# Eight output tiles instead of four in the first group of each MLP's up projection

## The chip, the cores and the metric

The kernel runs on one core of a Trainium2 chip. The metric is the device time of one execution in microseconds; smaller is better. Three executions of the kernel before took 2712.76 us (median), 2692.44 us (lowest) and 2718.33 us (highest).

## The reference

One inference step of a small diffusion backbone with two trunk layers, on 128 context tokens and 128 latent tokens, all in float32 with a model width of 2048. Layer 0 mixes with differential attention and an RWKV-7 scan, layer 1 with a Conformer convolution; each is followed by a gated MLP with a depthwise convolution of width 3. Before each of the four blocks stands an RMSNorm with a shift and a scale, behind each a gate, and these come from the conditioning vectors (adaLN). Cut to what the change touches:

```python
def adaln(cvec, w, b):
    return (jax.nn.silu(cvec) @ w + b)[:, None, :]

def conv_ffn(h, w_up, w_dw, w_down):
    u = dwconv(h @ w_up, w_dw)
    gate, val = jnp.split(u, 2, axis=-1)
    return (jax.nn.silu(gate) * val) @ w_down

# per layer l
sh1, sc1, g1, sh2, sc2, g2 = jnp.split(adaln(c, w_ada[l], b_ada[l]), 6, axis=-1)
...
h = rmsnorm(x, norm_g[l, 1]) * (1.0 + sc2) + sh2
x = x + g2 * conv_ffn(h, w_up[l], w_ffn_dw[l], w_down[l])
```

w_up is 2048 x 11008 (5504 gate columns and 5504 value columns), w_down 5504 x 2048, w_ada 2048 x 12288 for each layer. The conditioning vector is a vector, so adaLN is two matrix-vector products per layer (one for the context, one for the latent tokens), and their cost is the reading of w_ada.

## The kernel before

Activations lie transposed: 128 features on the partitions, 256 columns (128 context and 128 latent tokens). A float32 operand is split into a rounded part and a remainder, so each product of a 128 x 128 weight tile with the input of one k-tile takes three matmuls of 256 columns: weight times input, weight times the input's remainder, and the weight's remainder times input (lines 252, 254, 255).

**The weight stream.** All big weights go through one stream (`emit_load`, lines 175 to 198). SyncE issues the DMAs into a ring of seven raw buffers of 1024 columns (line 188), ScalarE copies one into the weight buffer (line 192), VectorE, or GpSimd in the convolution layer, makes the remainder (line 194). There are four weight buffers of 1024 columns each. A load holds as many k-tiles as fit: two for a group of four tiles (512 columns), one for a group of eight (1024).

**A matrix product** (`gemm`, line 235) runs over its plan's groups of output tiles. For each group it takes PSUM banks (two tiles to a bank, seven banks in all), runs over the k-tiles, and for each k-tile does all tiles of the group. After each k-tile it lets waiting evacuations advance by two steps (`pump`) and calls `fill`, a hook for other work. When the group is done, its evacuation is put on the list of pending work, to be stepped during the next group.

**The MLP** (`ffn`, line 1519) is four products: up for the first 22 of 43 feature tiles (gate and value tiles of a group together), down over these 22 k-tiles, up for the other 21, and down over them. A group of an up projection has two gate and two value tiles. Its evacuation (`up_evac`, line 1523) copies each tile from PSUM with the middle tap (line 1530), adds the two other taps on VectorE (line 1535), and then makes SiLU, the product (line 1543) and the two parts of the result (lines 1545 and 1550). The buffers of line 1529 hold eight tiles.

**The input of the up projection** (`modulated`, line 558) is made one k-tile at a time while the first group runs, at most two k-tiles ahead of it: two instructions on VectorE at line 572, two on ScalarE at line 575, two on VectorE at line 577.

**The adaLN vectors** are made in small steps by one generator, `ada_gen` (line 463), in a fixed order: for layer 0 shift and scale of the mixer, gate g1, sc2, sh2, gate g2, then for layer 1 sc1, sh1, g1, sc2, sh2, g2, each but the first two in two halves of 1024 columns with 16 loads of 512 KB of w_ada. There are two ways. `ada_vec` (line 426) multiplies on VectorE, two products of 128 x 1024 per load (lines 444 and 446), one product to a call; a half takes 38 calls: one for the first load, 32 with a product, three empty, one for 16 small matmuls (line 454) and one for the transpose and the end. It is used for layer 0's g2, layer 1's sc1, sh1, g2 and the first half of layer 1's g1. `ada_pe` (line 392) uses TensorE (line 421); in layer 1 a call takes two loads, and a half takes ten calls: one that only loads, eight with matmuls, of which seven load as well, and one for the end. Both take raw buffers from the same ring and DMAs from the same SyncE queue as the weight stream.

Calls are handed out by counting k-tiles in `fill`. In the output projection of layer 0 every fourth k-tile of 28 makes a call (line 1511). In layer 0's MLP it is every second one after the sixteenth, through all four products, until the first half of layer 1's g1 is done (line 1572; k-tiles before the last four of a product with `tail=4` count). In the convolution layer's first projection (144 k-tiles) it is every fourth after the sixteenth (line 1671), and while its last evacuations drain one call a round (line 1683). Its second projection (line 1734) has no fill. In layer 1's MLP it is every second one after the sixteenth (line 1741). Where a vector is needed, `ada_until` (line 491) hands out all calls that are missing, in one block: for layer 1's sc2 and sh2 that is line 1736, between the second projection and the MLP's input.

The order that the code gives is a priority. A planner with a cost model sorts the instructions of all engines at build time and may draw work ahead when it is ready, but a raw buffer goes to the next load in order.

Of the kernel before, what the change touches and what calls it, by code (L numbers as in the profile page):

```python
# [82 lines left out]
def tile_step(ctx: ExitStack, tc: tile.TileContext, A):  # L83
# [499 lines left out]
    def view_for(wap):  # L583
        def load(eng, dst, g, kt, na):
            pieces, w = g["pieces"], g["w"]
            n = len(pieces)
            step = pieces[1] - pieces[0] if n > 1 else wap.shape[1]
            src = wap[:, 0:n * step].rearrange("(k p) (m y) -> p k m y", p=P, m=n)
            src = src[:, kt:kt + na, :, pieces[0]:pieces[0] + w]
            dst = dst.rearrange("p (a m x) -> p a m x", a=na, m=n)  # L590
            if n < na:
                for m in range(n):
                    eng.dma_start(out=dst[:, :, m], in_=src[:, :, m])
            else:
                for a in range(na):
                    eng.dma_start(out=dst[:, a], in_=src[:, a])
        return load

    def grp(pieces, w, tiles, **kw):
        return dict(pieces=pieces, w=w, n=len(pieces) * w, tiles=tiles, **kw)  # L600
# [23 lines left out]
    def ffn_plans(l):  # L624
        def ups(a, b):
            gs = []
            i = a
            while i < b:
                n = min(2, b - i)
                gs.append(grp([i * P, DFF + i * P], n * P, [P * j for j in range(2 * n)], i=i, n_=n))  # L630
                i += n
            return Plan(view_for(A["w_up"][l]), gs, list(range(KT)))

        def downs(a, b):
            return Plan(view_for(A["w_down"][l]), full, list(range(a, b)))
        return [ups(0, HALF), downs(0, HALF), ups(HALF, FT), downs(HALF, FT)]
# [1169 lines left out]
```

## Time and profile before

| | |
|---|---|
| median of three executions | 2712.76 us |
| the profiled execution, its own time | 2696.26 us |
| span of its instructions | 2694.4 us |
| mean granted clock of TensorE | 0.978 |
| TensorE busy (matmul) | 96% of the span |
| VectorE busy | 75% |
| ScalarE busy | 47% |
| GpSimd busy | 11% |
| DMA | 616.58 MB, 229 GB/s over the span |

In the profile PE is TensorE's matmuls and PEld its weight loads, DVE VectorE, ACT ScalarE, POOL GpSimd, SP SyncE with its DMA queue. A row of an engine's instructions in order of time has the start, the length, engine and line, the operation, the tile written and the tiles read, the shape, how many instructions are merged, and in brackets how long the engine sat idle before it and what ended that. Tiles go by their names in the code: `raw` is a raw buffer, `wbt` the weight buffers, `hbt` the modulated input of a product, `mm` a PSUM bank, `u` the MLP's inner activation, `av` the sums of an adaLN half on VectorE, `cu` the convolution's sums. A table of stretches gives, for each, its length, the busy time of the engines with the number of instructions that started, the granted clock, the DMA share and the rate in GB/s. Layer 0's MLP runs from 819.65 us to about 1575, the convolution layer from there to 1931.5, layer 1's MLP from about 1970 to 2674.

### The profile page before, as it was taken

How to read it: one execution, taken by the hardware profiler on the slowest of the kernel's cores; microseconds unless marked ns; L12 is line 12 of the kernel's file. 1: busy time of each engine (PE TensorE's matmuls, PEld its weight loads, DVE VectorE, ACT ScalarE, POOL GpSimd, SP SyncE). 2: the span in 40 equal slices, each digit the busy share in tenths (PEclk: the TensorE clock that was granted, in tenths of full speed). 3: DMA queues.
4: the chain of work that ended last, by engine and by line, in shares of the span. 5: the costliest groups of instructions: out<-in, count | busy, mean ns of one | idle time of the engine just before them, and what ended most of it. 6: DMA issues, size and time to landing. Idle time of an engine off the chain costs nothing.

```text
span 2694.4 us, 60352 instructions
## 1 busy us (share of the span) xinstructions
PE 2599.1 (96%) x24347; PEld 2436.0 (90%) x24347; DVE 2031.0 (75%) x3460; ACT 1258.8 (47%) x2063; POOL 300.5 (11%) x313
## 2 busy tenths in 40 slices
PE   6999998999998999999999989999999999999998
PEld 5898996667898999999999989978889999999998
DVE  3667755676579898888999989995579985566655
ACT  4335544545345444434444453355444443355544
POOL 2000112011100000000000057753200000000000
PEclk9999999999799999999999999999999999999999
DMA  9996666656366887877878857875798876666663
GB/s 299 340 290 189 190 182 233 215 197 219 109 192 195 250 269 246 275 250 248 278 248 264 273 173 245 293 233 163 245 309 267 259 234 194 193 194 196 193 190 118
DMA packets 421368, 616.58 MB, mean 229 GB/s; under 512 B 32437, under 2 KB 291864, under 8 KB 420448
## 3 DMA queue, kind: packets, MB, share of 16 engines
q1 hardware_dynamic: 416688, 600.83, 70.1%
q0 software_dynamic: 3040, 6.57, 0.7%
q10 hardware_dynamic: 1360, 5.33, 0.5%
q8 instruction: 191, 3.13, 0.5%
q14 instruction: 89, 0.73, 0.1%
HBM read 604.75 MB, written 7.86 MB: 227 GB/s over the span
## 4 chain that ended last, share of the span: by engine, by line
PE 80%; DVE 5%; DMA 3%; ACT 1%; issue 1%; POOL 1%; SPq 1%; DVEq 0%; ACTq 0%; POOLq 0%
PE mm L252 22%; PE mm L255 22%; PE mm L254 22%; PE ada L421 3%; DMA raw<-in_w_ada 2%; PE mm L1078 1%; DMA raw<-in_w_up 1%; DVE cu L1646 1%; DVE wbt L194 1%; PE mm L1639 1%; PE mm L1111 1%; DVE av L446 1%; PE mm L1115 0%; PE ada L454 0%; PE mm L1273 0%
## 5 line engine op out<-in xcount | busy, mean ns | idle before, releaser
L192 ACT ACTIVATE wbt<-raw 128x1024 fp32r<-128x1024 f32 (+3 forms) x768 | 795.2, 1037 | 1032.0 <-PE mm L254 714.6
L252 PE MATMUL mm<-hbt,wbt 128*128 128x256 f32 x3888 | 1087.5, 282 | 6.0 <-ACT hbt L575 2.3
L254 PE MATMUL mm<-hbt,wbt 128*128 128x256 f32 x3888 | 1082.3, 280 | 3.2 <-DVE hbt L577 3.2
L194 DVE TENSOR_TENSOR wbt<-raw,wbt 128x1024 fp32r<-128x1024 f32 (+1 forms) x688 | 814.0, 1189 | 351.8 <-ACT wbt L192 343.1
L255 PE MATMUL mm<-hbt,wbt 128*128 128x256 f32 x3888 | 1065.1, 281 | 5.5 <-DVE wbt L194 5.3
L252 PEld LDWEIGHTS mm<-hbt,wbt 128*128 128x128 f32 x3888 | 734.3, 189 | 20.6 <-issue 9.2
L254 PEld LDWEIGHTS mm<-hbt,wbt 128*128 128x128 f32 x3888 | 734.6, 189 | 7.3 <-DVE hbt L577 5.2
L255 PEld LDWEIGHTS mm<-hbt,wbt 128*128 128x128 f32 x3888 | 723.5, 189 | 11.2 <-DVE wbt L194 6.6
L254 PE MATMUL mm<-u,wbt 128*128 128x256 f32 x1344 | 371.3, 278 | 0.0
L252 PE MATMUL mm<-u,wbt 128*128 128x256 f32 x1344 | 371.1, 278 | 0.0
L255 PE MATMUL mm<-u,wbt 128*128 128x256 f32 x1344 | 366.0, 278 | 0.0
L446 DVE SCALAR_TENSOR_TENSOR av<-raw,silu_c,av 128x1024 f32<-128x1024 f32 x270 | 337.4, 1280 | 32.6 <-DMA raw<-in_w_ada 32.4
L194 POOL TENSOR_TENSOR wbt<-raw,wbt 128x1024 fp32r<-128x1024 f32 x80 | 193.8, 2431 | 908.5 <-ACT wbt L192 905.7
L252 PEld LDWEIGHTS mm<-u,wbt 128*128 128x128 f32 x1344 | 252.2, 188 | 0.4 <-issue 0.4
L254 PEld LDWEIGHTS mm<-u,wbt 128*128 128x128 f32 x1344 | 252.1, 188 | 0.4 <-issue 0.4
L255 PEld LDWEIGHTS mm<-u,wbt 128*128 128x128 f32 x1344 | 249.2, 188 | 0.4 <-issue 0.4
L421 PE MATMUL ada<-raw,silu_c 128*32 128x256 f32 (+2 forms) x2688 | 157.3, 338 | 31.6 <-DMA raw<-in_w_ada 25.2
L1646 DVE SCALAR_TENSOR_TENSOR cu<-mm,vec,cu 128x256 f32<-128x256 f32 x428 | 174.9, 474 | 2.3 <-ACT cu L1630 1.0
L1535 DVE SCALAR_TENSOR_TENSOR cv<-mm,vec,cv 128x254 f32<-128x254 f32 x344 | 147.5, 475 | 12.6 <-ACT cv L1530 12.6
L421 PEld LDWEIGHTS ada<-raw,silu_c 128*32 128x32 f32 x2688 | 68.0, 114 | 87.8 <-issue 28.1
L286 PE MATMUL mm<-hbt,wbt 128*128 128x256 f32 x448 | 131.6, 298 | 0.4 <-ACT hbt L575 0.4
L288 PE MATMUL mm<-hbt,wbt 128*128 128x256 f32 x448 | 127.1, 285 | 0.3 <-DVE hbt L577 0.3
(442 smaller groups left out, 2800.0 us busy)
## 6 DMA issues: line engine op xcount, KB each, us to landing
raw<-in_w_ada SPq DMA_DIRECT2D x384, 512.0 KB, 5.4
raw<-in_w_up SPq DMA_DIRECT2D x688, 256.0 KB, 4.2
raw<-in_w_down SPq DMA_DIRECT2D x168, 512.0 KB, 5.0
raw<-in_w_pw SPq DMA_DIRECT2D x128, 256.0 KB, 4.3
raw<-in_w_in SPq DMA_DIRECT2D x64, 384.0 KB, 5.7
raw<-in_w_in SPq DMA_DIRECT2D x48, 512.0 KB, 3.8
raw<-in_w_out SPq DMA_DIRECT2D x32, 512.0 KB, 4.0
raw<-in_w_pw SPq DMA_DIRECT2D x32, 512.0 KB, 4.7
```

The lines of the kernel that those rows point to most:

```text
L192: act.activation(w[:, 0, 0:na * n], v, AF.Copy)
L194: pl.lo(pl.count).tensor_tensor(out=w[:, 1, 0:na * n], in0=v, in1=w[:, 0, 0:na * n].bitcast(F32), op=ALU.subtract)
L252: pe.matmul(ps, lhsT=hi, rhs=r[:, 0:TT], start=(ki == 0 and (nl > 0 or j % 2 == 0)), stop=False, skip_group_check=True)
L254: pe.matmul(ps, lhsT=hi, rhs=r[:, TT:2 * TT], start=False, stop=False, skip_group_check=True)
L255: pe.matmul(ps, lhsT=lo, rhs=r[:, 0:TT], start=False, stop=(ki == nk - 1), skip_group_check=True)
L286: pe.matmul(ps, lhsT=hi, rhs=r[:, 0:TT], start=(ki == 0 and j % 2 == 0), stop=False, skip_group_check=True)
L288: pe.matmul(ps, lhsT=hi, rhs=r[:, TT:2 * TT], start=False, stop=False, skip_group_check=True)
L421: pe.matmul(ps[32 * j:32 * j + 32, 0:nb * 32], lhsT=silu_c[:, kt, :], rhs=rv[:, j], start=(kt == 0), stop=(kt == KT - 1))
L446: dve.scalar_tensor_tensor(out=av[:, s], in0=raw, scalar=sc, in1=av[:, s], op0=ALU.mult, op1=ALU.add)
L1078: pe.matmul(dst_[h][:, s * TT:(s + 1) * TT], lhsT=src[pr, s], rhs=kr[pr, s].rearrange("p a t -> p (a t)"), start=True, stop=True)
L1535: dve.scalar_tensor_tensor(out=o[:, :, a_], in0=v2(ps)[:, :, b_], scalar=w(k, ct), in1=o[:, :, a_], op0=ALU.mult, op1=ALU.add)
L1646: dve.scalar_tensor_tensor(out=o, in0=pads[a](k), scalar=V("w_dw", k * KT + ct), in1=o, op0=ALU.mult, op1=ALU.add)
```

## The change

The first group of the first up projection of each layer's MLP (feature tile 0) takes four gate and four value tiles. The nine groups behind it keep two and two, so the plan has ten groups for its 22 feature tiles where it had eleven. A load of the first group holds one k-tile of 1024 columns, one DMA of 512 KB with pieces of 512 columns, where it held two k-tiles of 512 columns in two DMAs of 256 KB with pieces of 256.

```diff
             while i < b:
-                n = min(2, b - i)
+                n = 4 if i == 0 else min(2, b - i)
                 gs.append(grp([i * P, DFF + i * P], n * P, [P * j for j in range(2 * n)], i=i, n_=n))
                 i += n
```

## The prediction

> **What bounds the kernel now.** I read the page's totals first, then engine busy time by stretch, then TensorE's instructions in order of time for idle before them, last SyncE's queue and VectorE in the same stretches.
>
> ```profile
> span 2694.4 us, 60352 instructions
> PE 2599.1 (96%) x24347; PEld 2436.0 (90%) x24347; DVE 2031.0 (75%) x3460; ACT 1258.8 (47%) x2063; POOL 300.5 (11%) x313
> ...
> L194 DVE TENSOR_TENSOR wbt<-raw,wbt 128x1024 fp32r<-128x1024 f32 (+1 forms) x688 | 814.0, 1189 | 351.8 <-ACT wbt L192 343.1
> ...
> L446 DVE SCALAR_TENSOR_TENSOR av<-raw,silu_c,av 128x1024 f32<-128x1024 f32 x270 | 337.4, 1280 | 32.6 <-DMA raw<-in_w_ada 32.4
> ```
> ```profile
> 815.00:1076.00 261.00, 255.10 (x2130) 251.28 (x2131) 241.61 (x344) 130.12 (x201) 0.00 (x0) 0.98 0.77 240
> ...
> 1838.00:1931.50 93.50, 93.32 (x772) 93.18 (x774) 54.89 (x95) 51.16 (x78) 41.05 (x22) 0.97 0.55 169
> 1931.50:1970.00 38.50, 28.28 (x300) 14.07 (x299) 13.03 (x48) 7.56 (x21) 0.00 (x0) 0.87 0.96 358
> 1970.00:2192.00 222.00, 221.96 (x1876) 220.78 (x1880) 213.98 (x278) 113.48 (x167) 0.00 (x0) 0.99 0.85 271
> ...
> 1860.00:1900.00 40.00, 40.00 (x342) 40.00 (x341) 20.81 (x31) 17.35 (x23) 18.96 (x9) 1.00 0.62 190
> ```
> Columns of the second fence: stretch and length, busy PE, PEld, DVE, ACT, POOL with counts, granted clock, DMA share, GB/s. TensorE is the bound nearly everywhere: 342 matmuls in 40 us are 0.117 us each, so a k-step of four tiles (12 matmuls) takes 1.40 us, of eight (24) 2.81 us, a group of four tiles 22.5 us. VectorE is close behind in the up projections (242 of 261 us and 214 of 222). One stretch is different: 1931.5 to 1970, where TensorE issues only 300 matmuls while DMA is at 0.96.
>
> ```profile
> 1931.50:1967.70 36.20, 18.69 (x240) 5.93 (x240) 0.89 0.95 359
> ```
> This is the same table for line 421 alone: the block between the convolution layer's second projection and layer 1's MLP is filled by 240 small adaLN matmuls.
>
> What can the first group of an up projection lose today? In layer 0 it starts at 819.65, in layer 1 in earnest at 1969.87:
>
> ```profile
> 819.65 0.79 PE L252 MATMUL mm<-hbt,wbt 128*128 128x256 f32 x2 [1.17 <-ACT hbt L575]
> 820.74 0.58 PE L254 MATMUL mm<-hbt,wbt 128*128 128x256 f32 x1 [0.30 <-DVE hbt L577]
> 840.18 0.39 PE L254 MATMUL mm<-hbt,wbt 128*128 128x256 f32 x1 [0.54 <-DVE hbt L577]
> 857.00 0.39 PE L255 MATMUL mm<-hbt,wbt 128*128 128x256 f32 x1 [2.65 <-DVE wbt L194]
> 1969.87 0.58 PE L252 MATMUL mm<-hbt,wbt 128*128 128x256 f32 x1 [1.58 <-ACT wbt L192]
> ```
> The waits after the start are 0.30 + 0.54 us for the modulated input and 2.65 us for a weight split: 3.5 us in layer 0. In layer 1 TensorE is busy 221.96 of 222.00 us after 1970. So there is little to win here.
>
> **The change part by part.** *Matmuls.* Their number and shapes stay; 16 steps of 24 replace 32 of 12: 0.
>
> *Start of the group.* The input of k-step kt is made while the group runs:
>
> ```profile
> 831.47 0.60 DVE L572 SCALAR_TENSOR_TENSOR ht<-x,Acoef,mm 128x128 f32<-128x128 f32 x2
> 831.99 0.87 DVE L577 SCALAR_TENSOR_TENSOR hbt<-ht,adaT,hbt 128x128 fp32r<-128x128 f32 x3
> ...
> 851.41 2.48 DVE L446 SCALAR_TENSOR_TENSOR av<-raw,silu_c,av 128x1024 f32<-128x1024 f32 x2 [1.96 <-DMA raw<-in_w_ada]
> ...
> 856.86 1.65 DVE L1535 SCALAR_TENSOR_TENSOR cv<-mm,vec,cv 128x254 f32<-128x254 f32 x4
> ...
> 863.86 0.76 DVE L1543 TENSOR_TENSOR cv<-cv 128x256 f32<-128x256 f32 x2
> ```
> Two instructions of 0.30 and two of 0.29 us a step are 1.18 us; half a weight split (1.19) makes 1.78 us against TensorE's 1.40, so VectorE falls behind by 6 us over the group, most of which the prefetched weights cover. With eight tiles it is 1.18 + 1.19 = 2.37 against 2.81: the waits for the input go. The 2.65 us stand behind an adaLN product (L446) that waited 1.96 us for its weights and kept the split at L194 waiting; the fill begins only after 16 k-steps, which are now 45 us long, so it moves away from the crowded start. I take -3.0 (bounds 0 and -3.5); in layer 1 nothing.
>
> *Loads.* Sixteen w_up DMAs of 512 KB replace 32 of 256 KB, with the same bytes per matmul; both forms fill the same four weight buffers, and before the group both stop at two loads ahead (48 matmuls): 0.
>
> *Evacuation.* All eight tiles come due in the second group: 16 of L1535 at 0.41, eight of L1543/L1550's size at 0.38, eight splits at 1.19 and 6.7 adaLN products at 1.28 make 27.7 us of VectorE in 22.5 us of TensorE (22.9 before). The cover is the lead that VectorE wins in the first group, 16 x 0.44 = 7 us: 0, and 5.2 us per layer if the lead is gone. Four banks of seven are held then, and the second group needs two: 0.
>
> *Fewer k-steps.* The up projection's first plan has 160 k-steps instead of 176, and adaLN work is handed out by counting k-steps. Layer 0's MLP has 520 now and 504 then; every second one after the sixteenth makes a step: 252 and 244. With 7 from the output projection that is 259 and 251 calls. A VectorE part takes 38 calls, so layer 0's g2 and layer 1's sc1 and sh1 (228) still fit, but layer 1's g1 first half (to 266) now lacks 15 calls instead of 7. The convolution's first projection offers (144 - 16) / 4 = 32 calls and about 6 more while it drains; what is over comes as one block after its second projection, since that has no fill. The queue bears the count out:
>
> ```profile
> 1550.81 0.34 SPq L434 DMA_DIRECT2D raw<-in_w_ada  x1
> ...
> 1624.75 3.17 SPq L402 DMA_DIRECT2D raw<-in_w_ada  x2
> ...
> 1793.93 18.46 SPq L402 DMA_DIRECT2D raw<-in_w_ada  x10
> ...
> 1905.54 5.32 SPq L596 DMA_DIRECT2D raw<-in_w_up  x4
> 1911.57 48.67 SPq L402 DMA_DIRECT2D raw<-in_w_ada  x30
> 1960.33 17.37 SPq L596 DMA_DIRECT2D raw<-in_w_up  x20
> ```
> 32 + 6 - 7 = 31 calls at ten per part with 16 loads are three parts and one call: 50 of the 80 loads, 30 left, as the x30 row shows. Eight calls fewer are 23: two parts and three calls, 38 loads, 42 left. So the block grows by 12 loads of 512 KB, ahead of the MLP's own weights in SyncE's queue. Its price, from TensorE's rows (the first is of the chain that ended last):
>
> ```profile
> 1931.53 3.20 PE ada L421 x56
> ```
> ```profile
> 1939.27 0.64 PE L421 MATMUL ada<-raw,silu_c 128*32 128x256 f32 x8 [0.60 <-DMA raw<-in_w_ada]
> 1940.53 0.64 PE L421 MATMUL ada<-raw,silu_c 128*32 128x256 f32 x8 [0.62 <-DMA raw<-in_w_ada]
> 1941.80 0.64 PE L421 MATMUL ada<-raw,silu_c 128*32 128x256 f32 x8 [0.64 <-DMA raw<-in_w_ada]
> 1943.08 1.08 PE L421 MATMUL ada<-raw,silu_c 128*32 128x256 f32 x8 [0.64 <-DMA raw<-in_w_ada]
> ...
> 1967.20 1.08 PE L421 MATMUL ada<-raw,silu_c 128*32 128x256 f32 x8 [0.66 <-DMA raw<-in_w_ada]
> ```
> A load (eight matmuls) comes every 1.27 us and is waited for: 12 x 1.27 = +15.2. The block's mean is dearer: seven loads (x56) fit ahead of 1931.5, one for each raw buffer, and the other 23 take until 1967.2, with the pauses at the block's start and end: 1.55 each, +18.6. I take the steady spacing, since a longer block has the same start and end; bounds 15.2 and 18.6, and 0 if the loads slip into the projection before it.
>
> The Trainium skill, "DMA: Bandwidth & Descriptors", Specifications, gives some 358 GB/s of HBM per core; 12 loads would then be an estimated 17.6 us and the sum 2.4 us higher. The rows at 1.27 us are 413 GB/s, above that figure; "Perfetto Trace Analysis", Roofline, of the Trainium skill allows a core that runs alone about 435 GB/s, by which it would be an estimated 14.5 us. The trace agrees with the second.
>
> *The eight calls that move into the convolution.* They are eight L446 products: 10.2 us of VectorE, and their four loads go between w_pw loads on SyncE. What waits behind them on VectorE are the taps of the convolution. VectorE's third column there:
>
> ```profile
> 1600.00:1620.00 20.00, 19.84 (x169) 19.64 (x169) 14.32 (x32) 10.83 (x13) 18.85 (x9) 1.00 0.57 186
> ...
> 1640.00:1660.00 20.00, 20.00 (x184) 18.57 (x183) 18.55 (x45) 7.93 (x10) 14.69 (x7) 1.00 0.81 257
> 1660.00:1680.00 20.00, 20.00 (x189) 17.85 (x189) 17.17 (x47) 7.92 (x10) 13.31 (x6) 1.00 0.86 281
> 1680.00:1700.00 20.00, 20.00 (x190) 17.85 (x189) 20.00 (x55) 7.83 (x10) 14.66 (x7) 1.00 0.89 287
> ```
> From 1680 on it is full and sets the stage's end; before lie 5.7 + 1.4 + 2.8 = 9.9 us of idle. All 10.2 fit or none: 0 to +10.2. One pair should fit the first hole and 4.3 us the others, which leaves 3.3; +3.0. TensorE drops eight calls of adaLN there, but is not the bound at the end: 0. In layer 1's MLP g2 needs 76 calls and gets 72; the last four are two empty ones, 16 small matmuls and a transpose, needed only at the first down evacuation: 0.
>
> **Sum.** -3.0 + 15.2 + 3.0 = +15.2 us. The profiled execution took 2696.26 us (span 2694.4), so 2711.5 by it. It lies 16.5 us under the median of the runs shown; the mean of it and the three runs is 2704.9, and from that I forecast 2720 us, 0.6% more than before. A measurement of this kernel tells about 1% (27 us) from no change, so this is "the same", leaning to slower.
>
> **Rivals.** *VectorE loses its lead* (slower, 0.17): the place is the second group of each up projection, the price 5.2 us twice, and it decides if the splits stand fewer than two loads ahead when the first group ends. For it: VectorE is busy 242 of 261 us. Against: 7 us of slack in the new first group. No gain at the start, so 15.2 + 3.0 + 10.4 = +28.6: 2733.
> *The convolution takes none of the products into its holes* (0.15): 15.2 + 10.2 - 3.0 = +22.4: 2727. For it, 20.00 of 20 us from 1680; against, the holes before.
> *The late loads are hidden* (0.12): the scheduler draws them into the second projection, where DMA is at 0.55. For it: it already runs adaLN work ahead of its place, as the chain's row
>
> ```profile
> 1568.41 1.04 PE ada L454 x16
> ```
> shows, the reduction of g1's first half, which the code hands out only in the convolution's projection, from 1577 on. Against: no w_ada load left before the last w_pw load, as the seven raw buffers hold weights. Then only the start's gain stays, -3.5 at most: 2701.
> *The start gains nothing* because VectorE paces both forms: +18.2, 2723; inside the forecast.
>
> **How the numbers follow.** Forecast 0.56, the rivals 0.17, 0.15 and 0.12. From 2701 less and 2733 more some 5 to 14 us of scatter between executions (2692.44 to 2718.33): 2696 to 2747. Slower by over 1%: half of the first rival, a third of the second, and 0.1 from scatter on the forecast: 0.23. Faster by over 1% would need 27 us where all waits of the first groups are 3.5: 0.05. Same: 0.72.
>
> **What would show it.** Right: some 42 w_ada loads in one run of SyncE's queue before layer 1's MLP and its first weight matmul in earnest some 15 us later after the second projection than now; no wait on L577 in layer 0's first group; eight more L446 after 1560, before the convolution's taps are done. Wrong: a block of 30 again; or waits on L194 in the second group; or a first group that gains more than 3.5 us.

## The result and the profile after

The kernel after took 2733.92 us (median of five executions, 2732.35 to 2741.54); beside it the kernel before took 2696.17 us (2691.8 to 2718.33). The ratio over all executions (not simply that of the two medians) is 1.0127 with an interval of 1.0088 to 1.0165: slower by 1.3%. The time lies in the range of the forecast, but the sum of +15.2 us was less than half of what came. The profiled execution after took 2741.54 us with a span of 2739.8, 45.4 us longer than the span before. It is the longest of its five, 7.6 us above their median, so the stages below add up to more than the 37.8 us between the medians. From the page after, the span, the totals and the group of adaLN products:

```profile
span 2739.8 us, 60288 instructions
PE 2628.8 (96%) x24347; PEld 2460.3 (90%) x24347; DVE 2036.4 (74%) x3460; ACT 1259.3 (46%) x2063; POOL 303.0 (11%) x313
...
L446 DVE SCALAR_TENSOR_TENSOR av<-raw,silu_c,av 128x1024 f32<-128x1024 f32 x270 | 345.3, 1303 | 36.7 <-DMA raw<-in_w_ada 36.7
```

The matmuls are the same 24347, and TensorE is "busy" 29.7 us longer with them. VectorE does its 3460 instructions in 5 us more. So most of the loss isn't idle time, and the busy column alone doesn't find it. Cut at landmarks of TensorE's instructions in order of time, both profiled executions divide like this (us; layer 1's MLP ends with the last matmul of its last down product, at 2680.9 before and 2726.3 after):

| stage | before | after | difference | forecast |
|---|---|---|---|---|
| up to the first up matmul of layer 0 | 819.65 | 820.74 | +1.1 | 0 |
| layer 0's MLP, to the norm's first matmul (L518) | 751.6 | 745.3 | -6.3 | -3.0 |
| norm and convolution, to the second projection | 267.0 | 282.0 | +15.0 | +3.0 |
| second projection | 93.1 | 93.1 | 0 | 0 |
| block of adaLN loads | 38.6 | 55.0 | +16.4 | +15.2 |
| layer 1's MLP | 711.1 | 730.2 | +19.2 | 0 |

The landmarks after, from TensorE's rows (start, us, engine, line, then the idle time before the row and its releaser):

```profile
820.74 1.22 PE L252 MATMUL mm<-hbt,wbt 128*128 128x256 f32 x4 [1.17 <-ACT hbt L575]
...
1847.97 0.79 PE L252 MATMUL mm<-hbt,wbt 128*128 128x256 f32 x2 [2.05 <-ACT hbt L537]
...
1996.05 0.58 PE L252 MATMUL mm<-hbt,wbt 128*128 128x256 f32 x1 [1.59 <-ACT wbt L192]
```

The second projection began at 1838.18 before:

```profile
1838.18 0.80 PE L252 MATMUL mm<-hbt,wbt 128*128 128x256 f32 x2 [2.05 <-ACT hbt L537]
```

**The first group** of layer 0 no longer waits behind its start, on L577 or on L194. All waits of TensorE between 820 and 1076 us after (total, count, longest):

```profile
PE mm L252 <- ACT hbt L575: 1.2, 1, 1.2
```

**The block** is as forecast. SyncE's queue after, then the table of stretches there:

```profile
1921.40 65.23 SPq L402 DMA_DIRECT2D raw<-in_w_ada  x42
```
```profile
1941.00:1996.00 55.00, 41.29 (x398) 16.85 (x396) 13.67 (x50) 7.50 (x22) 0.00 (x0) 0.76 0.96 364
```

(The columns are those of the prediction's tables.) 42 loads in one run instead of 30, with DMA at 0.96, and 16.4 us more of it.

**Layer 1's MLP** lost 19.2 us although TensorE has no gap in it in either kernel. Count the matmuls of one stretch, far from the change; after, then before:

```profile
2380.00:2420.00 40.00, 40.00 (x342) 40.00 (x342) 24.72 (x35) 19.88 (x29) 0.00 (x0) 1.00 0.62 185
```
```profile
2380.00:2420.00 40.00, 40.00 (x355) 40.00 (x354) 26.51 (x39) 20.92 (x31) 0.00 (x0) 1.00 0.62 191
```

Both show TensorE busy 40.00 of 40 us at a granted clock of 1.00, but 342 matmuls went through against 355. Fitted over longer stretches, one matmul of the weight stream takes 0.1178 us in the one and 0.1133 in the other. In the profile before, the faster pace begins where the small adaLN matmuls (128*32) cut into the stream for the last time, and holds from there to the last down product's end, to 2673:

```profile
2085.55 1.07 PE L454 MATMUL ada<-av,sel 128*32 128x256 f32 x16
...
2191.81 0.64 PE L454 MATMUL ada<-av,sel 128*32 128x256 f32 x8
...
2194.94 0.64 PE L454 MATMUL ada<-av,sel 128*32 128x256 f32 x8
```

After, the sixteen matmuls of the first half no longer come in one piece, and the slower pace stays:

```profile
2134.47 0.64 PE L454 MATMUL ada<-av,sel 128*32 128x256 f32 x8
...
2140.89 0.64 PE L454 MATMUL ada<-av,sel 128*32 128x256 f32 x8
...
2243.42 0.64 PE L454 MATMUL ada<-av,sel 128*32 128x256 f32 x8
...
2248.07 0.64 PE L454 MATMUL ada<-av,sel 128*32 128x256 f32 x8
```

0.1178 is 4.0% more than 0.1133, and 4.0% of the last 478 us are 19.0 of the 19.2 us. Executions of one kernel mostly fall into two clusters about 20 us apart (of 29 executions of the kernel before, 21 took 2688 to 2700 us and eight 2709 to 2724), which is about the price of this pace, though no execution of the longer cluster was traced; a median must be read with that.

**The convolution** lost 15.0 us. VectorE's groups of instructions between 1559 and 1700 us (count, busy us and mean ns, idle before and its releaser), after, then before:

```profile
L446 DVE SCALAR_TENSOR_TENSOR av<-raw,silu_c,av 128x1024 f32<-128x1024 f32 x8 | 16.4, 2079 | 6.7 <-DMA raw<-in_w_ada 6.7
...
L472 DVE TENSOR_TENSOR adaT<-atr,vec 128x16 f32<-128x16 f32 x1 | 8.5, 8462 | 0.0
```
```profile
L446 DVE SCALAR_TENSOR_TENSOR av<-raw,silu_c,av 128x1024 f32<-128x1024 f32 x1 | 1.3, 1291 | 0.0
```

The eight products that the prediction named are there, at 2079 ns a product instead of 1280, with 6.7 us of waiting for their loads. In order of time, VectorE after:

```profile
1571.97 2.48 DVE L446 SCALAR_TENSOR_TENSOR av<-raw,silu_c,av 128x1024 f32<-128x1024 f32 x2 [1.45 <-DMA raw<-in_w_ada]
...
1614.13 5.47 DVE L446 SCALAR_TENSOR_TENSOR av<-raw,silu_c,av 128x1024 f32<-128x1024 f32 x2 [3.49 <-DMA raw<-in_w_ada]
...
1627.36 5.66 DVE L446 SCALAR_TENSOR_TENSOR av<-raw,silu_c,av 128x1024 f32<-128x1024 f32 x2 [0.58 <-DMA raw<-in_w_ada]
...
1665.78 4.76 DVE L1664 TENSOR_TENSOR acc<-acc,cu 128x256 f32<-128x256 f32 x1
...
1686.72 8.46 DVE L472 TENSOR_TENSOR adaT<-atr,vec 128x16 f32<-128x16 f32 x1
```

and GpSimd's weight splits after:

```profile
1615.59 8.70 POOL L194 TENSOR_TENSOR wbt<-raw,wbt 128x1024 fp32r<-128x1024 f32 x3 [0.44 <-ACT wbt L192]
...
1676.00 19.16 POOL L194 TENSOR_TENSOR wbt<-raw,wbt 128x1024 fp32r<-128x1024 f32 x8 [5.74 <-ACT wbt L192]
```

A pair takes 2.48 us where GpSimd stands still and over 5 us beside its splits (the fourth pair, between the first two rows, found gaps between splits and took 1.29 and 1.49). The smallest instruction in the picture, 128 x 16 elements at L472, is recorded with 8.46 us: it ends at 1695.18, and GpSimd's run of eight splits ends at 1695.16. The Trainium skill ("SBUF — State Buffer", SBUF: two separate sides) states that a VectorE instruction with two operands in SBUF and a GpSimd instruction that reads SBUF take one pair of ports in turn, the other waiting for all of it. The trace agrees, and shows more: the small instruction waited through about 3.5 splits that followed each other without a gap (8.46 over 2.40 us). In calls_lost and layer1_calls_8 (below) the same instruction took 8.42 and 8.48 us and ended within 0.05 us of a run of eight splits too. The taps at L1646, which read one operand from PSUM (`mm`), don't wait: here are their count, smallest, median and largest ns between 1640 and 1700 us, beside the same splits.

```profile
L1646 DVE SCALAR_TENSOR_TENSOR cu<-mm,vec,cu x116: 443/472/475, 1639.6 to 1699.8; 128x256 f32<-128x256 f32 x116
```

What stands behind VectorE is ScalarE's first tap (L1630), which needs VectorE's L1622. The waits between 1575 and 1850 us (total, count, longest), after, then before:

```profile
ACT cu L1630 <- DVE mm L1622: 28.2, 5, 11.8
```
```profile
ACT cu L1630 <- DVE mm L1622: 3.2, 7, 0.7
```

And the longest of them, in ScalarE's order of time after, followed by SyncE's queue and TensorE:

```profile
1710.41 0.56 ACT L1630 ACTIVATE cu<-mm,vec 128x256 f32<-128x256 f32 x1 [11.85 <-DVE mm L1622]
1710.88 1.04 ACT L192 ACTIVATE wbt<-raw 128x1024 fp32r<-128x1024 f32 x1
```
```profile
1702.95 0.81 SPq L402 DMA_DIRECT2D raw<-in_w_ada  x2
1714.42 3.56 SPq L596 DMA_DIRECT2D raw<-in_w_pw  x4
```
```profile
1711.97 0.39 PE L252 MATMUL mm<-hbt,wbt 128*128 128x256 f32 x1 [1.80 <-ACT wbt L192]
...
1714.45 0.58 PE L255 MATMUL mm<-hbt,wbt 128*128 128x256 f32 x1 [1.97 <-POOL wbt L194]
...
1728.30 0.58 PE L252 MATMUL mm<-hbt,wbt 128*128 128x256 f32 x1 [2.83 <-ACT cg L1618]
```

The weight copy (L192) stands in ScalarE's queue behind the waiting tap, so no raw buffer comes free, SyncE issues no load for 10.7 us (1703.76 to 1714.42), and TensorE starves 1.80 + 1.97 us for weights and 2.83 us for a ScalarE instruction (L1618) that stood behind a late copy. The tap before had been let go at 1674 us after a wait of 7.47 us: the held-back weight copies came in a bunch, GpSimd's splits followed without gaps (the x8 row began after a wait of 5.74 us for L192), and L472 waited for the rest of that bunch.

### The profile page after: what moved, and what is told of

Same layout as the page of the kernel before. It is cut to its first block, busy times and chain, and to the rows that moved or that the text cites. A ratio compares the mean times of both kernels' runs of the same rounds, so it can differ in the third digit from the quotient of the medians.

```text
span 2739.8 us, 60288 instructions
## 1 busy us (share of the span) xinstructions
PE 2628.8 (96%) x24347; PEld 2460.3 (90%) x24347; DVE 2036.4 (74%) x3460; ACT 1259.3 (46%) x2063; POOL 303.0 (11%) x313
## 5 line engine op out<-in xcount | busy, mean ns | idle before, releaser
L192 ACT ACTIVATE wbt<-raw 128x1024 fp32r<-128x1024 f32 (+3 forms) x768 | 794.6, 1036 | 1043.2 <-PE mm L254 713.9
L194 DVE TENSOR_TENSOR wbt<-raw,wbt 128x1024 fp32r<-128x1024 f32 (+1 forms) x688 | 814.9, 1189 | 376.2 <-ACT wbt L192 368.1
L446 DVE SCALAR_TENSOR_TENSOR av<-raw,silu_c,av 128x1024 f32<-128x1024 f32 x270 | 345.3, 1303 | 36.7 <-DMA raw<-in_w_ada 36.7
L194 POOL TENSOR_TENSOR wbt<-raw,wbt 128x1024 fp32r<-128x1024 f32 x80 | 197.2, 2485 | 914.4 <-ACT wbt L192 912.4
L1646 DVE SCALAR_TENSOR_TENSOR cu<-mm,vec,cu 128x256 f32<-128x256 f32 x428 | 173.0, 470 | 0.9
```

The source lines that it names most:

```text
L192: act.activation(w[:, 0, 0:na * n], v, AF.Copy)
L194: pl.lo(pl.count).tensor_tensor(out=w[:, 1, 0:na * n], in0=v, in1=w[:, 0, 0:na * n].bitcast(F32), op=ALU.subtract)
L446: dve.scalar_tensor_tensor(out=av[:, s], in0=raw, scalar=sc, in1=av[:, s], op0=ALU.mult, op1=ALU.add)
L1646: dve.scalar_tensor_tensor(out=o, in0=pads[a](k), scalar=V("w_dw", k * KT + ct), in1=o, op0=ALU.mult, op1=ALU.add)
```

## The experiments

The theory to be tested: all of the loss comes from adaLN calls that are handed out by counting k-tiles; eight tiles in a group cost nothing themselves. The rival: the larger group itself slows the up projections, for instance through its held banks, its larger loads, or the evacuation of eight tiles.

| kernel | loads in the block | norm and convolution | block | layer 1's MLP | median us | ratio to before (interval) |
|---|---|---|---|---|---|---|
| before | 30 | 267.0 | 38.6 | 711.1 | | |
| after | 42 | 282.0 | 55.0 | 730.2 | 2733.92 | 1.0127 (1.0088 to 1.0165) |
| calls_kept | 30 | 269.2 | 39.7 | 711.7 | 2686.06 | 0.996 (0.9926 to 0.9993) |
| calls_lost | 42 | 279.4 | 52.9 | 731.1 | 2741.74 | 1.0156 (1.0121 to 1.0192) |
| layer1_only | 30 | 268.8 | 38.8 | 730.3 | 2712.14 | 1.0049 (1.0024 to 1.0074) |
| p2_fill | 0 | 273.2 | 7.6 | 717.3 | 2692.0 | 0.9969 (0.9943 to 0.9994) |
| layer1_calls | 30 | 269.4 | 38.5 | 712.0 | 2693.58 | 0.9985 (0.996 to 1.0011) |
| late_g2 | 30 | 269.2 | 40.0 | 730.4 | 2714.86 | 1.0046 (1.0022 to 1.0071) |
| conv_only | 30 | 276.1 | 39.7 | 711.7 | 2704.32 | 1.0026 (0.9999 to 1.0054) |
| block_only | 42 | 255.3 | 54.6 | 730.6 | 2716.78 | 1.0057 (1.0031 to 1.0084) |
| first_tap_dve | 42 | 284.0 | 54.4 | 729.7 | 2736.1 | 1.0127 (1.0082 to 1.0171) |
| layer1_calls_8 | 42 | 288.1 | 56.5 | 712.1 | 2719.18 | 1.0075 (1.0046 to 1.0104) |
| early_calls | 16 | 283.1 | 19.0 | 710.9 | 2705.6 | 1.0027 (0.9996 to 1.0058) |
| small_products | 42 | 258.6 | 54.6 | 730.9 | 2723.56 | 1.0088 (1.0034 to 1.0141) |

The stages are those of each kernel's profiled execution. One trace of a stage isn't exact: where the convolution makes the calls of before (before, calls_kept, layer1_only, layer1_calls, late_g2) it takes 267.0 to 269.4 us, with the calls of after (after, calls_lost, layer1_calls_8) 279.4 to 288.1.

**calls_kept: eight tiles, but a k-tile of eight tiles makes two calls.**

```diff
-                    fill()
+                    for _ in range(max(1, nt // 4)):
+                        fill()
```

> The changed kernel, but a k-step of eight tiles calls the fill twice, so that as many adaLN calls are handed out as before. Theory A (the lost calls cost): the block before layer 1's MLP is back at 30 w_ada loads and the convolution stage at its length of before; only the start of layer 0's MLP gains some 3 us: 2690 to 2697 us where the last 480 us run at 0.113 us a matmul, 2709 to 2715 where they run at 0.118. Rival B (the eight tiles themselves cost: evacuation, weights, banks): 2725 to 2740 again, block of 30 or not.

The block is back at 30 loads, the convolution and layer 1's MLP are where they were, and layer 0's MLP takes 741.2 us, 10.4 less than before (part of it at the faster pace). The loss is gone and a gain of 0.4% stays, barely clear of nothing by its interval: this version beats both kernels. The rival falls. SyncE's block in it:

```profile
1902.61 50.30 SPq L403 DMA_DIRECT2D raw<-in_w_ada  x30
```

**calls_lost: the kernel before, with four-tile groups, and the same calls taken away.**

```diff
-                if cnt[0] % 2 == 0 and cnt[0] > 16 and (1, "g1", 0) not in ada_done:
+                if cnt[0] % 2 == 0 and cnt[0] > 32 and (1, "g1", 0) not in ada_done:
```

> The kernel before with four tiles everywhere, but layer 0's MLP hands out its first adaLN call after 32 k-steps instead of 16, so that eight calls are lost there as in the changed kernel. Theory A: 42 w_ada loads in the block, 16 us longer, and the convolution stage 12 to 15 us longer: 2722 to 2730 us where the last 480 us run at 0.113 us a matmul, 2740 to 2750 where they run at 0.118. Rival B: as before, 2692 to 2718.

All of the loss comes without a single eight-tile group: 42 loads, +12.4 in norm and convolution, +14.3 in the block and +20.0 in layer 1's MLP. Here too the pace of layer 1 is the slower one; its code is that of before, but its small matmuls cut in at other places (see layer1_calls and late_g2).

**layer1_only: eight tiles in layer 1 alone.**

```diff
-                n = 4 if i == 0 else min(2, b - i)
+                n = 4 if i == 0 and l == 1 else min(2, b - i)
```

> Eight tiles in layer 1's first group only; layer 0 as before, so no call is lost ahead of the block. Theory A: block of 30 and convolution as before; layer 1's MLP as before but for its pace, which theory C takes for chance at an interruption by the small adaLN matmuls: 2692 to 2718 us, in two clusters some 18 us apart. Rival D (the later end of g2 in layer 1, which the change brings, holds the last 480 us at 0.118 us a matmul): 2712 to 2720 in every execution, and 0.118 in the trace after 2200 us.

Block and convolution are as before, as they must be, since layer 0 makes its old calls; layer 1's MLP is 19.2 us longer. So layer 1 has a loss of its own, without a gap on any row of TensorE.

**layer1_calls: the same, with two calls per k-tile of eight tiles.**

```diff
-                    fill()
+                    [fill() for _ in range(max(1, nt // 4))]
```

> Eight tiles in layer 1's first group only, but with the fill called twice at its k-steps, so that g2's small matmuls fall where they fall in the kernel before. Theory D (the pace of the last 480 us is set by where these matmuls cut into the stream, with chance): mostly 2690 to 2698 us, some executions 18 us more, as in the kernel before; 0.113 us a matmul after 2200 us in most. Rival B (the eight tiles hold the slow pace): 2705 to 2717 in all executions, as when the calls are not kept.

**late_g2: the kernel before, its layer 1 calls beginning 16 k-tiles later.**

```diff
-                if cnt[0] % 2 == 0 and cnt[0] > 16:
+                if cnt[0] % 2 == 0 and cnt[0] > 32:
```

> Four tiles everywhere; layer 1's MLP hands out its first adaLN call after 32 k-steps instead of 16, so that g2 ends eight calls late as in the changed kernel. Theory D: 2709 to 2718 us in all executions, 0.118 us a matmul to the end. Rival B: as before, two of three executions at 2690 to 2698.

The two settle that it is the calls' place and not the group. The table of stretches of layer1_calls, then of late_g2:

```profile
2380.00:2420.00 40.00, 40.00 (x356) 40.00 (x355) 26.42 (x39) 20.98 (x31) 0.00 (x0) 1.00 0.64 192
```
```profile
2380.00:2420.00 40.00, 40.00 (x342) 40.00 (x341) 25.70 (x38) 20.22 (x30) 0.00 (x0) 1.00 0.62 184
```

Eight tiles with the old calls run at 0.113 us a matmul, four tiles with later calls at 0.117. All twelve executions of late_g2 and all twelve of layer1_only took longer than 2704 us, 11 of the 12 of layer1_calls less than 2701.

The places where small matmuls of L454 interrupt the stream in layer 1 sort all fourteen traces. Where g2's first sixteen small matmuls come in one piece and its last sixteen as eight and eight (before, calls_kept, p2_fill, layer1_calls, conv_only, layer1_calls_8, early_calls), the end runs at the faster pace; where the first sixteen are divided, it runs at the slower one. That holds for calls_lost and block_only too, where layer 1's code is untouched; in order of time in block_only:

```profile
2084.26 0.64 PE L454 MATMUL ada<-av,sel 128*32 128x256 f32 x8
...
2087.85 0.62 PE L454 MATMUL ada<-av,sel 128*32 128x256 f32 x2
...
2096.61 0.63 PE L454 MATMUL ada<-av,sel 128*32 128x256 f32 x6
...
2194.42 0.64 PE L454 MATMUL ada<-av,sel 128*32 128x256 f32 x8
...
2197.46 0.64 PE L454 MATMUL ada<-av,sel 128*32 128x256 f32 x8
```

There the faster pace begins at 2194.42 and ends at 2197.46. Of 40 times that it began at such an interruption in these traces, it ended at the very next one 33 times; the other seven had none behind them, and it lasted to the end of the last down product.

**block_only: the kernel before, the convolution's calls beginning 32 k-tiles later,** so that eight calls on TensorE fall out of the convolution into the block, and no product moves into it.

```diff
-                    if cnt[0] % 4 == 0 and (1, "sh2") not in ada_done and cnt[0] > 16:
+                    if cnt[0] % 4 == 0 and (1, "sh2") not in ada_done and cnt[0] > 48:
```

> Four tiles, layer 0 as before; the convolution's first projection hands out its first call after 48 k-steps instead of 16, so that eight TensorE calls move into the block and no product into the convolution. Theory A: 42 loads in the block, 16 us more there; the convolution stage 0 to 8 us shorter, as TensorE does eight calls less: 2703 to 2711 us at the fast pace, 2721 to 2729 at the slow one. Rival (the block grows only together with a convolution that is late): block as before, 2692 to 2718.

The block alone: 42 loads, +16.0. And a term that the prediction had at 0: eight TensorE calls fewer make norm and convolution 11.7 us shorter. So the eight products cost 26.7 us there (282.0 - 255.3), of which 11.7 were given back, as far as single traces tell.

**conv_only: the kernel before, with the eight products moved into the convolution and its calls handed out more closely, so that the block stays.**

```diff
-                if cnt[0] % 2 == 0 and cnt[0] > 16 and (1, "g1", 0) not in ada_done:
+                if cnt[0] % 2 == 0 and cnt[0] > 32 and (1, "g1", 0) not in ada_done:
...
-                    if cnt[0] % 4 == 0 and (1, "sh2") not in ada_done and cnt[0] > 16:
+                    if cnt[0] % (2 if cnt[0] <= 48 else 4) == 0 and (1, "sh2") not in ada_done and cnt[0] > 16:
```

> Four tiles; layer 0's MLP loses eight calls, as in the changed kernel, but the convolution's first projection hands out eight more in its place (every second k-step up to 48), so that the block stays at 30 loads. Theory A (eight products of 1.28 us on VectorE ahead of the taps cost 12 to 15 us in the norm and the convolution, apart from the block): the stretch from the end of layer 0's MLP to the second projection 9 to 15 us longer, block as before, 2703 to 2710 us at the fast pace and 2721 to 2728 at the slow one. Rival (the forecast's 3 us hold, and the rest belongs to the block's growth): 2695 to 2700 and 2713 to 2718.

The block stays at 30, norm and convolution lose 9.1 us, with the waits of the first tap at

```profile
ACT cu L1630 <- DVE mm L1622: 9.3, 5, 4.0
```

The same eight products are cheaper here: they are done by 1615 us instead of 1633, and L472, which follows them, met a GpSimd with pauses and took 1.37 us instead of 8.46. The price of a moved instruction is no property of the instruction alone.

**small_products: after, with the eight products on 8 of their 1024 columns.** It leaves out the rest of the multiplication for k-tiles 12 to 15 of that half; loads and calls stay.

```diff
-                    dve.scalar_tensor_tensor(out=av[:, s], in0=raw, scalar=sc, in1=av[:, s], op0=ALU.mult, op1=ALU.add)
+                    c8 = slice(0, 8 if (l, nm, b0) == (1, "g1", 0) and kt > 11 else 1024); dve.scalar_tensor_tensor(out=av[:, s, c8], in0=raw[:, c8], scalar=sc, in1=av[:, s, c8], op0=ALU.mult, op1=ALU.add)
```

> The changed kernel, in which the eight adaLN products that fall into the convolution (g1, first half, k-tiles 12 to 15) work on 8 of their 1024 columns, so that 10 us of VectorE's work is left out while their loads, waits and places in the order stay. Theory A (VectorE's work decides there): from the norm after layer 0's MLP to the second projection 255 to 268 us instead of 282.0. Rival H (the products' waits for their loads and the later TensorE calls decide): 275 us or more. Block of 42 in both.

Norm and convolution fall by 23.4 us to 258.6: by these two traces 23.4 of the 26.7 us come from VectorE's time in these products and what it sets off. The size is less sure than the direction: the traced execution is the shortest of four here (2712.39 us) and the longest of five after, and the medians lie only 10.4 us apart, though all four took less than any of the five. The remaining 3.3 us (their loads among w_pw's, or the calls) aren't taken apart. Even at 8 columns a pair can wait, in VectorE's order of time:

```profile
1588.44 4.18 DVE L446 SCALAR_TENSOR_TENSOR av<-raw,silu_c,av 128x8 f32<-128x8 f32 x2 [0.68 <-DMA raw<-in_w_ada]
...
1667.66 0.16 DVE L472 TENSOR_TENSOR adaT<-atr,vec 128x16 f32<-128x16 f32 x1
```

4.18 us for two instructions of eight columns isn't arithmetic; and L472 takes 0.16 us in a pause of GpSimd.

**first_tap_dve: after, with the first tap (L1630) moved from ScalarE to VectorE,** so that no weight copy can stand behind it.

```diff
-                        act.activation(v2(u[:, ct]), pads[a](0), AF.Identity, scale=V("w_dw", ct),
-                                       bias=V("b_dw", ct))
+                        dve.tensor_scalar(out=v2(u[:, ct]), in0=pads[a](0), scalar1=V("w_dw", ct),
+                                          scalar2=V("b_dw", ct), op0=ALU.mult, op1=ALU.add)
```

> The changed kernel with the convolution's first tap (line 1630) on VectorE instead of ScalarE. Theory E (with VectorE late, ScalarE waits at that tap, the weight copies stand behind it, and TensorE starves near 1710 us): the waits for that tap and TensorE's 7 us of gaps there go, and the convolution stage is some 3 to 7 us shorter than in the changed kernel's 272.5, although VectorE does 16 instructions of some 0.45 us more. Rival F (VectorE's sum of work alone sets the stage): 5 to 8 us longer.

Neither number came: norm and convolution took 2.1 us more, which is less than such traces differ by. TensorE's gaps near 1710 fell from 6.6 us to 0.9, so the queue behind the tap is real, but nothing was won: VectorE took over 16 taps of 0.53 us, and TensorE's waits from 1760 us to just before the second projection grew from 8.6 to 16.5 us. That fits a stage in which VectorE is what is short and ScalarE's wait only passes it on; this run alone doesn't show it.

**layer1_calls_8: after, with two calls per k-tile in layer 1's first up projection only.**

```diff
-                    fill()
+                    [fill() for _ in range(2 if nt == 8 and plan is p_f1[0] else 1)]
```

> The changed kernel with the fill called twice at the eight-tile k-steps of layer 1 only. Theory D (where g2's small matmuls cut into the stream sets the pace of the rest): 0.113 us a matmul from 2220 us on in most executions, 2712 to 2722 us, 18 less than the changed kernel. Rival G (the bigger block, which also shifts the order of work in layer 1, holds the slow pace by itself, as in the two four-tile kernels with a block of 42): 2730 to 2742 us.

Layer 1's MLP comes back to 712.1 us while block and convolution keep their losses, so the two are separate. One pair of products took 10.17 us in this convolution, beside the second half of a run of eight splits on GpSimd, and L472 8.48, which goes with its 288.1.

**Two tries to go beyond calls_kept** missed. p2_fill gives the second projection a fill, so that no adaLN load is left for the block:

```diff
-                gemm(p_p2, lambda kt: hc[:, kt], residual(1, "g1", acc), tail=4)
+                cnt[0] = 0
+
+                def fill_p2():
+                    cnt[0] += 1
+                    if cnt[0] % 3 == 0 and (1, "sh2") not in ada_done:
+                        ada_step()
+                gemm(p_p2, lambda kt: hc[:, kt], residual(1, "g1", acc), fill_p2, tail=4)
```

> As the kernel with the calls kept, and the convolution's second projection gets a fill, a call at every third k-step (20 calls, 19 needed). Theory A: the block before layer 1's MLP, 38 us in the kernel before, shrinks to the 10 us or so of the norm; the second projection takes in 30 loads at 0.5 us of TensorE each, +15: 10 to 15 us faster than the kernel with the calls kept. Rival: the loads hold up the projection's weights on the same queue (62 loads at 1.27 us are 79 of its 94 us), and nothing is won.

The block shrank by 32 us against calls_kept, but the second projection grew by 15.9 (it now carries the small matmuls), norm and convolution by 4.0 and layer 1's MLP by 5.6, whose first matmuls had run during the block. No gain against calls_kept: 2692.0 against 2686.06.

early_calls (on top of calls_kept) lets layer 0's MLP make calls from its second k-tile on:

```diff
-                if cnt[0] % 2 == 0 and cnt[0] > 16 and (1, "g1", 0) not in ada_done:
+                if cnt[0] % 2 == 0 and (1, "g1", 0) not in ada_done:
```

> The kernel with the calls kept, and layer 0's MLP hands out adaLN calls from its first k-step: eight more, so that g1's first half ends in layer 0's MLP and the block falls to 16 w_ada loads. Theory A: block 18 us shorter, the convolution some 9 to 12 us longer for eight TensorE calls more, VectorE's 7 us of slack in the first group spent on eight products (0 to 4 us of waits): 2 to 8 us faster than the kernel with the calls kept, 2672 to 2684 us. Rival: the products at the start bring the waits for the modulated input back, and nothing is won: 2684 to 2692.

The block fell to 16 loads and 19.0 us. But norm and convolution, with eight more TensorE calls in them, grew by 13.9 us against calls_kept, and the planner drew products ahead into the end of the output projection, so that the norm's sum waited there, in TensorE's order of time:

```profile
824.58 0.56 PE L518 MATMUL mm<-ones,acc 128*128 128x2 f32 x2 [11.82 <-DVE acc L507]
```

Layer 0's first up matmul came at 833.6 instead of 819.3 in calls_kept.

## Why the prediction was right in some steps and wrong in others

**The count of calls and the block: right.** 42 loads were forecast and 42 came; 12 x 1.27 = 15.2 us were forecast, 16.4 measured, 16.0 in block_only. The bounds of 15.2 and 18.6 hold both; calls_lost, with 14.3, lies just below.

**The start of the group: right in its size.** The waits of 3.5 us in layer 0's first group are gone. The other 3 of the 6.3 us are pace: between 1063.73 and 1149.28 us the kernel after ran at the faster one, and 4.0% of 85 us are 3.4. In layer 1 nothing was forecast and nothing came.

**Loads and evacuation at 0: right.** With the calls restored, eight tiles cost nothing: calls_kept gains a little (0.996), layer1_calls (0.9985) can't be told from before. The first rival, that VectorE loses its lead, is thereby out, and the trace after has no wait on L194 in the second groups, which was its sign.

**The step that failed first: "One pair should fit the first hole and 4.3 us the others, which leaves 3.3; +3.0".** It came to +15.0. The mechanism was named, its size was off in three ways. A product was priced at 1.28 us, from rows where GpSimd does nothing; in the convolution it shares its time with the splits and took 2.08 on average. The products' own waits for loads, 6.7 us, fill holes too and weren't counted. And behind VectorE the prediction saw only the taps there, not ScalarE's first tap with the weight copies behind it (28.2 us of waits instead of 3.2). Against that stands a gain that it put at 0 because TensorE wasn't the bound at the end: 11.7 us from eight TensorE calls fewer. By single traces the term is -11.7 + 23.4 + 3.3 = +15.0; its middle part may be smaller (see small_products). The second rival, +10.2 for the convolution, came nearest.

**The step that failed second: "In layer 1's MLP g2 needs 76 calls and gets 72; the last four are two empty ones, 16 small matmuls and a transpose, needed only at the first down evacuation: 0".** The count is right and no wait came of it. What it didn't see is that the way the small matmuls cut into the weight stream also goes with the pace afterwards: +19.2 us, the largest term of all. The profile before had it in sight: 342 matmuls in 40 us at 1860, which the prediction quotes and divided by, and 355 at 2380, which it never counted. One rate was taken for the whole kernel.

**The number: luck.** The base of 2704.9 us lies 8.7 us above the 2696.17 beside the result, and it made the forecast of 2720 look nearer than the sum was. The range reached 2733.92 only because its upper end stood on the first rival, with its 2733, and scatter; that rival's mechanism didn't come. By the prediction's own line of 1% the ratio of 1.0127 falls to "slower", which it gave 0.23, though the interval reaches below that line.

**Open:** why an interruption changes the pace, and why some begin the faster one and others don't. Their pattern goes with it in all fourteen traces, but single executions of one kernel differ in time, and no run moves one interruption and nothing else. That L472's 8.46 us come from GpSimd's run of splits is read from coinciding ends in three traces, from its 0.16 to 1.37 us where GpSimd pauses, and from the taps that don't wait; no run isolates it.

## What to carry to other kernels

When a change alters the number of steps of a loop, look for everything that is handed out by counting those steps, and keep the count: with it this change gained 0.4%, barely clear of nothing, without it it cost 1.3%. Price a moved instruction by rows from the place where it goes, beside the engines that run there, and look at what stands behind it on every engine that waits for it. And where an engine is "busy" all the time in both profiles, compare its counts per stretch, not its busy share.

## What the runs showed of the hardware that was not expected

The weight stream runs at one of two paces, 0.1178 or 0.1133 us a matmul, at the same granted clock of 1.00; a faster stretch that begins where 128*32 matmuls of L454 interrupt it ends at their next interruption (33 of 33 times), or lasts for up to 480 us where none follows. Some shorter ones begin elsewhere.

A VectorE instruction with two SBUF operands can wait for a whole run of GpSimd splits: 8.46 us for 128 x 16 elements. The same product takes 1.28 us between 900 and 1500 us, where GpSimd does nothing; the row of the view by tile of the kernel before gives smallest, median and largest ns:

```profile
L446 DVE SCALAR_TENSOR_TENSOR av<-raw,silu_c,av x163: 1270/1280/1289, 902.8 to 1498.3; 128x1024 f32<-128x1024 f32 x163
```
